# A hybrid attention and retention step on one core: where the opening stage applies the gain of its first normalisation

## The chip, the core and the metric

The kernel runs on one core of a Trainium2 chip. A core has a matrix engine (PE, TensorE), three engines that work on 128 partitions at a time (DVE, ACT and POOL: VectorE, ScalarE and GpSimd), and an engine (SP) that does little here but issue transfers. 16 DMA engines move data between the HBM and the on-chip memory SBUF. PE writes its results to PSUM, another on-chip memory, from where DVE or ACT take them; POOL works on SBUF alone. The metric is the device time of one execution in microseconds; less is better. Three runs of the kernel before had a median of 2458.14 us (2456.72 to 2460.6).

## The reference

One layer for 1024 frames of one new stream (the prompt) and 16 frames each of 8 running streams (the samples, 128 rows together). The model width is 2048; there are 8 heads of 128 for each of two branches.

```python
def rms_norm(x, g):
    y = xf * rsqrt(mean(xf * xf, axis=-1) + EPS)
    return y * g

h = rms_norm(x, norm_pre)              # (frames, 2048)
p = einsum('btd,de->bte', h, w_in)     # w_in: 2048 x 8192
q_sb, k_sb, v_sb, gate_sb, q_r, k_r, v_r, gate_r = split(p)
q_r, k_r = rope(q_r), rope(k_r) * HEAD_DIM ** -0.5
o_sb = stick_breaking_block(...)       # attention, strictly causal, over past and new keys
o_r, s = retention(...)                # 64-frame chunks and a running state
y = concat(head_norm(o_sb) * silu(gate_sb), head_norm(o_r) * silu(gate_r))
x + rms_norm(y @ w_out, norm_post)
```

The change touches only the first line of it: the mean square of a row of x, its inverse root, and the product with the 2048 gains `norm_pre`, which are the same for all rows and differ along the width.

## The kernel before

**Tiles and groups.** Nine tiles of 128 rows: eight of the prompt (0 to 7) and one of the samples (8). Group 0 holds tiles 0, 1, 2, 3 and the samples (640 columns once they are turned), group 1 tiles 4 to 7. All projections of group 0 run first, then those of group 1, then the output projection. Each projection needs h turned, with the width on the partitions: 16 blocks of 128x128 per tile.

**Products.** Both operands of a product are split into a high part (rounded by the ACT copy to the matrix engine's fp32r type) and a low part (DVE subtracts the high part from the source): `split`, L127 to L129. Three products, high by high, high by low and low by high, make one (`products`, L216 to L232; `project_rows`, L247 on). The turned and split h lies in `mov`: four parts for the width, each a pair `mh` and `ml`. The weights come as blocks `wr` of 256 KB through four buffers and are split in the same way into `wh` and `wl` (`load_w`, L207).

**The opening stage** (L335 to L402) makes `mov` for group 0:

1. `load_x` fetches a tile of x, 1 MB, into one of four buffers `xt`. The first tile is asked for first, then the gains, `norm_pre` spread over all 128 partitions as `gpre` (1 MB in two halves), then two more tiles, then the four weight blocks of the first projection, then the last two tiles. All go through SP's queue.
2. `stats` (L371): ACT squares the tile and sums the squares (`mean_square`, L350); seven small instructions on DVE and ACT make the inverse root (`inv_rms`, L131 to L142: p0v, p0r, p0u). For the first four tiles this becomes a diagonal matrix `dg` (L377); for the samples the tile itself is multiplied by it (L384).
3. Also in `stats`, the tile is multiplied by `gpre`, in eight pieces of 256 columns (L380): on POOL for tiles 1, 2 and 3 (`PRE_POOL` gives positions in the group), on DVE for tile 0 and the samples.
4. `turn` (L354): PE turns four blocks into one PSUM bank `p0t`, by a product with `dg` (L360), which scales the rows at the same time and is recorded as two instructions per block, or by a plain transpose (L358), one per block. There are four such banks.
5. `split` takes the bank apart into `mov`: ACT writes `mh`, DVE writes `ml`, both from PSUM.

After the second tile the first projection's products for the first 256 columns (L225 on 128x256) stand in the program, after all five those for the remaining 384 columns. The other columns of this first head, and `project_rows` with its blocks `wrn`, `whn`, `wln`, follow.

**Group 1** is prepared beside these products by `stage_rest` (L410 to L424), a job that moves on a step each time the products have ticked far enough: a tile is loaded and squared, one DVE instruction multiplies it by root and gains (L417), PE turns it, ACT copies the bank to `hs` (L422), and `hs` is stored in HBM for later.

**Order.** The program is traced in the order of the code, and a planner then orders each engine's instructions: it takes what its own model of the machine holds for ready, the earlier traced first. On the chip each engine keeps to that order. So an instruction that waits holds up all behind it on its engine.

Of the kernel before, what the change touches and what calls it, by code (L numbers as in the profile page):

```python
# [9 lines left out]
F32 = mybir.dt.float32  # L10
F32R = mybir.dt.float32r
AF = mybir.ActivationFunctionType
ALU = mybir.AluOpType
# [3 lines left out]
P = 128  # L17
D = 2048
KT = D // P
# [5 lines left out]
NT = PT + 1  # L25
SAMPLE = PT
WQ = 4
PRE_POOL = (1, 2, 3)
PRE_DIAG = (0, 1, 2, 3)
PRE_CUT = 8  # L30
PRE_G = 2
D_REST = 8
KC_AHEAD = 2
D_DEC = 2
# [23 lines left out]
def tile_hybrid_step(  # L58
# [26 lines left out]
    nc = tc.nc  # L85
# [12 lines left out]
    def x_rows(t):  # L98
        return x_prompt[0, t * P : (t + 1) * P, :] if t < PT else xs_flat
# [10 lines left out]
    ident = const.tile([P, P], F32, name="ident")  # L110
# [16 lines left out]
    def split(hi, lo, src):  # L127
        nc.scalar.activation(hi, src, AF.Copy)  # L128
        nc.vector.tensor_tensor(lo, src, hi.bitcast(F32), ALU.subtract)  # L129

    def inv_rms(pool, ssq, n, name):  # L131
        shape = list(ssq.shape)
        v = pool.tile(shape, F32, name=f"{name}v")
        r = pool.tile(shape, F32, name=f"{name}r")
        u = pool.tile(shape, F32, name=f"{name}u")
        nc.vector.tensor_scalar(v, ssq, 1.0 / n, EPS, ALU.mult, ALU.add)
        nc.scalar.activation(r, v, AF.Sqrt)
        nc.vector.reciprocal(r, r)
        nc.vector.tensor_tensor(u, r, r, ALU.mult)
        nc.vector.tensor_tensor(u, u, v, ALU.mult)  # L140
        nc.vector.tensor_scalar(u, u, -0.5, 1.5, ALU.mult, ALU.add)
        nc.vector.tensor_tensor(r, r, u, ALU.mult)  # L142
        return r
# [41 lines left out]
    def drain(job):  # L185
        while job is not None and not job.done:
            tick()
# [4 lines left out]
    def moving(pool, n):  # L192
        return [list(x) for x in zip(*(moving_part(pool, n, q) for q in range(KT // WQ)))]
# [42 lines left out]
    def acc_banks(g):  # L236
        return [accp.tile([P, 512], F32, name=f"acc{i}", tag=f"acc{i}") for i in range(len(g["pieces"]))]
# [9 lines left out]
    col = lambda i, h: i * H * P + h * P  # L247
# [40 lines left out]
    with ExitStack() as s1:  # L288
# [46 lines left out]
        g0 = GROUPS[0]  # L335
        with tc.tile_pool(name="p0", bufs=2) as p0, tc.tile_pool(name="p0s", bufs=1) as p0s, tc.tile_pool(
            name="p0p", bufs=4, space=PSUM
        ) as p0p:
            warm = p0s.tile([P, 1], F32, name="warm")
            nc.scalar.activation(warm, eps, AF.Sqrt)  # L340

            def load_x(t):
                xt = p0.tile([P, D], F32, name="xt", tag="xt", bufs=4)
                nc.sync.dma_start(xt, x_rows(t))
                return xt

            def mean_square(xt):
                ssq = p0.tile([P, 1], F32, name="ssq", tag="ssq")
                sq = p0s.tile([P, D], F32, name="sq0", tag="sq0")
                nc.scalar.activation(sq, xt, AF.Square, accum_out=ssq)  # L350
                return inv_rms(p0, ssq, D, "p0")

            def turn(q, xt, scale=None):
                pt = p0p.tile([P, 4, P], F32, name="p0t", tag="p0t")  # L354
                for j in range(4):
                    blk = xt[:, (4 * q + j) * P : (4 * q + j + 1) * P]
                    if scale is None:
                        nc.tensor.transpose(pt[:, j, :], blk, ident)  # L358
                    else:
                        nc.tensor.matmul(pt[:, j, :], blk, scale, start=True, stop=True)  # L360
                return pt

            tiles = g0["tiles"]
            loaded = [load_x(tiles[0])]
            gpre = p0s.tile([P, D], F32, name="gpre")
            for c in range(PRE_G):
                cs = slice(c * D // PRE_G, (c + 1) * D // PRE_G)
                nc.sync.dma_start(gpre[:, cs], norm_pre[0, cs].partition_broadcast(P))
            loaded += [load_x(t) for t in tiles[1:3]]

            def stats(i):  # L371
                xt = loaded[i]
                rstd = mean_square(xt)
                dg = None
                if i in PRE_DIAG:
                    dg = p0.tile([P, P], F32, name="dg", tag="dg")
                    nc.vector.tensor_scalar(dg, ident, rstd, None, ALU.mult)  # L377
                for c in range(PRE_CUT):
                    cs = slice(c * D // PRE_CUT, (c + 1) * D // PRE_CUT)
                    (nc.gpsimd if i in PRE_POOL else nc.vector).tensor_tensor(  # L380
                        xt[:, cs], xt[:, cs], gpre[:, cs], ALU.mult
                    )
                if dg is None:
                    nc.vector.tensor_scalar(xt, xt, rstd, None, ALU.mult)  # L384
                return dg

            scales = [stats(0)]
            for i, t in enumerate(tiles):
                if i + 1 < len(tiles):
                    scales.append(stats(i + 1))  # L390
                cs = slice(i * P, (i + 1) * P)
                for q in range(KT // 4):
                    pt = turn(q, loaded[i], scales[i])
                    split(mov[0][q][:, :, cs], mov[1][q][:, :, cs], pt)
                if i == 1:
                    w4 = list(load_w(col(4, 0)))
                    loaded += [load_x(t) for t in tiles[3:]]
                    acc = acc_banks(g0)
                    for w in w4:
                        products(mov, acc[:1], g0["pieces"][:1], *w)  # L400
            for w in w4:
                last = products(mov, acc[1:], g0["pieces"][1:], *w)  # L402

            nc.sync.dma_start(dec, c_dec)
            load_rope(0)
            with nc.allow_non_contiguous_dma(reason="small gains"):
                nc.sync.dma_start(gains[:, 0, :], sb_gain[0].rearrange("(h p) -> p h", p=P))
                nc.sync.dma_start(gains[:, 1, :], ret_gain[0].rearrange("(h p) -> p h", p=P))

            def stage_rest():  # L410
                for i, t in enumerate(GROUPS[1]["tiles"]):
                    hs = p0s.tile([P, KT, P], F32, name="hs", tag="hs")
                    xt = load_x(t)
                    yield 6

                    rstd = mean_square(xt)
                    nc.vector.scalar_tensor_tensor(xt, xt, rstd, gpre, ALU.mult, ALU.mult)  # L417
                    yield 12
                    for q in range(KT // 4):
                        with tc.issue_after(last.ins) if q == 0 else nullcontext():  # L420
                            pt = turn(q, xt)
                        nc.scalar.activation(hs[:, 4 * q : 4 * q + 4, :], pt, AF.Copy)  # L422
                        yield 3
                    nc.scalar.dma_start(s_h[:, :, i * P : (i + 1) * P], hs)  # L424

            job = Job(stage_rest(), D_REST)
            first = ret_inputs(g0, mov, 0, list(zip(acc, g0["pieces"])))
            ret_values(g0, mov, 0)
            first = *first[:2], pair["r"][:, :, 0, :], dict(rg=gate(project(g0, mov, col(7, 0)), "rg"))
            drain(job)  # L430
# [692 lines left out]
```

## Time and profile before

| | |
|---|---|
| median of 3 runs | 2458.14 us |
| the profiled execution | 2452.19 us |
| its span, first to last instruction | 2450.5 us |
| PE busy | 2372.9 us, 97% |
| DVE, ACT, POOL busy | 1263.9, 915.1, 655.6 us |
| granted PE clock over the span | 0.988 |

The span is what the engines' instructions cover; 1.7 us of the profiled execution lie outside it, and that execution is 6 us shorter than the median. PE's idle time, 78 us in all, is what a faster order can win; in the profile a row of the timeline reads: start, duration, engine, line, operation, output and input tiles with their shapes, how many, and in brackets how long the engine had been idle and what ended that. In the table of stretches each row has the busy time of an engine in the stretch and, in brackets, its number of instructions; then the granted PE clock (1 is full), the busy share of the DMA engines and what they moved.

### The profile page before, as it was taken

To read this page: it belongs to the slowest core of one execution; us is meant where nothing else is said; L and a number is where in the kernel's file an instruction comes from. 1 tells how busy PE (TensorE), PEld (TensorE's weight loads), DVE (VectorE), ACT (ScalarE), POOL (GpSimd) and SP (SyncE) were. 2 spreads that over 40 slices of the span, in tenths; PEclk is the share of its full clock that TensorE was granted. 3 is DMA by queue.
4 is the path that set the end of the run, shared out by engine and by line. 5 is a ranking of instruction groups with operands and counts; after the bars stand their busy time and mean duration, and the time that the engine had idled before them with its cause. 6 is when DMAs were issued, how large, how long until landed. Compare 5 with 4: busy or idle time off the path is not lost.

```text
span 2450.5 us, 40488 instructions
## 1 busy us (share of the span) xinstructions
PE 2372.9 (97%) x14832; PEld 2100.2 (86%) x14832; DVE 1263.9 (52%) x2434; ACT 915.1 (37%) x1931; POOL 655.6 (27%) x1029
## 2 busy tenths in 40 slices
PE   7999999999999999999889999999999998999998
PEld 7998899989999899998678888898888877878787
DVE  7245445454555555456445454545545555564544
ACT  6332333333333333334333334333433443444333
POOL 2144253444344353444102112121111211000000
PEclk9999999999999999999989999999999999999999
DMA  7659789797979798797766565566556566665553
GB/s 239 169 126 217 149 188 178 172 198 152 198 157 210 156 201 165 177 206 181 175 161 150 136 145 158 135 149 160 133 138 150 152 147 169 226 221 189 185 183 133
DMA packets 674888, 418.67 MB, mean 171 GB/s; under 512 B 224512, under 2 KB 619776, under 8 KB 672256
## 3 DMA queue, kind: packets, MB, share of 16 engines
q1 hardware_dynamic: 524272, 285.99, 48.1%
q0 software_dynamic: 32256, 71.36, 13.5%
q10 hardware_dynamic: 118160, 58.74, 8.8%
q8 instruction: 116, 1.90, 0.4%
q14 instruction: 84, 0.69, 0.1%
HBM read 336.24 MB, written 79.69 MB: 170 GB/s over the span
## 4 chain that ended last, share of the span: by engine, by line
PE 70%; issue 12%; DMA 8%; DVE 6%; POOL 2%; ACT 1%; SPq 1%; DVEq 0%; ACTq 0%; POOLq 0%
PE acc L225 33%; PE accn L274 15%; PE a L944 4%; PE a L945 4%; PE a L943 4%; PE pa L596 2%; DMA kc<-cache_sb_k 2%; DMA wr<-w_in 1%; PE z L566 1%; PE zc L639 1%; POOL kc L623 1%; DMA mr<-s_y 1%; PE pa L686 1%; DMA ro<-s_rk 1%; DVE wl L129 1%
## 5 line engine op out<-in xcount | busy, mean ns | idle before, releaser
L225 PE MATMUL acc<-mh,wh 128*128 128x256 f32 (+2 forms) x2304 | 671.8, 344 | 3.0 <-ACT wh L128 2.8
L225 PE MATMUL acc<-mh,wl 128*128 128x256 f32 (+2 forms) x2304 | 661.5, 340 | 7.4 <-DVE wl L129 7.4
L225 PE MATMUL acc<-ml,wh 128*128 128x256 f32 (+2 forms) x2304 | 666.8, 342 | 0.0
L129 DVE TENSOR_TENSOR wl<-wr,wh 128x512 fp32r<-128x512 f32 (+1 forms) x576 | 394.1, 689 | 495.4 <-ACT wh L128 479.5
L128 ACT ACTIVATE wh<-wr 128x512 fp32r<-128x512 f32 (+1 forms) x576 | 356.5, 624 | 735.5 <-PE acc L225 335.9
L225 PEld LDWEIGHTS acc<-mh,wh 128*128 128x128 f32 x2304 | 419.2, 189 | 54.4 <-issue 16.6
L225 PEld LDWEIGHTS acc<-mh,wl 128*128 128x128 f32 x2304 | 425.5, 189 | 44.9 <-DVE wl L129 10.7
L225 PEld LDWEIGHTS acc<-ml,wh 128*128 128x128 f32 x2304 | 425.5, 189 | 36.5 <-issue 9.0
L623 POOL DMA_DIRECT2D kc<-cache_sb_k x512 | 332.4, 655 | 403.0 <-DVE kcT L648 220.9
L274 PE MATMUL accn<-whn,mh 128*128 128x256 f32 x1152 | 327.8, 287 | 3.0 <-ACT mh L128 2.9
L274 PE MATMUL accn<-wln,mh 128*128 128x256 f32 x1152 | 325.3, 283 | 2.5 <-DVE wln L129 2.5
L274 PE MATMUL accn<-whn,ml 128*128 128x256 f32 x1152 | 324.7, 283 | 0.0
L274 PEld LDWEIGHTS accn<-whn,mh 128*128 128x128 f32 x1152 | 219.8, 191 | 18.7 <-issue 11.7
L944 PE MATMUL a<-wl,mh 128*128 128x512 f32 (+1 forms) x576 | 220.2, 382 | 6.7 <-DVE wl L129 6.7
L274 PEld LDWEIGHTS accn<-wln,mh 128*128 128x128 f32 x1152 | 220.6, 191 | 4.2 <-DVE wln L129 3.9
L943 PE MATMUL a<-wh,mh 128*128 128x512 f32 (+1 forms) x576 | 219.0, 382 | 2.9 <-DVE sg L301 2.4
L274 PEld LDWEIGHTS accn<-whn,ml 128*128 128x128 f32 x1152 | 220.3, 191 | 0.3 <-DVE ml L129 0.2
L945 PE MATMUL a<-wh,ml 128*128 128x512 f32 (+1 forms) x576 | 220.4, 383 | 0.0
L129 DVE TENSOR_TENSOR wln<-wrn,whn 128x512 fp32r<-128x512 f32 x128 | 87.9, 698 | 108.9 <-ACT whn L128 104.9
L491 POOL TENSOR_SCALAR_AFFINE_SELECT kp<-kp 128x128 f32<-128x128 f32 x40 | 12.4, 311 | 472.2 <-ACT kp L485 472.1
L128 ACT ACTIVATE whn<-wrn 128x512 fp32r<-128x512 f32 x128 | 78.4, 636 | 161.4 <-PE acc L225 66.5
L944 PEld LDWEIGHTS a<-wl,mh 128*128 128x128 f32 x576 | 108.7, 189 | 29.4 <-DVE wl L129 8.8
(189 smaller groups left out, 2730.5 us busy)
## 6 DMA issues: line engine op xcount, KB each, us to landing
wr<-w_in SPq DMA_DIRECT2D x384, 256.0 KB, 4.4
wr<-w_out SPq DMA_DIRECT2D x184, 256.0 KB, 3.6
wrn<-w_in SPq DMA_DIRECT2D x128, 256.0 KB, 3.3
kc<-cache_sb_k POOLq DMA_DIRECT2D x512, 64.0 KB, 5.2
vc<-cache_sb_v SPq DMA_DIRECT2D x64, 512.0 KB, 9.0
xt<-x_prompt SPq DMA_DIRECT2D x8, 1024.0 KB, 5.6
xr<-x_prompt SPq DMA_DIRECT2D x8, 1024.0 KB, 6.2
out<-out ACTq DMA_DIRECT2D x12, 512.0 KB, 2.8
```

The costliest lines, as they stand in the source:

```text
L128: nc.scalar.activation(hi, src, AF.Copy)
L129: nc.vector.tensor_tensor(lo, src, hi.bitcast(F32), ALU.subtract)
L225: last = nc.tensor.matmul(a[:, :m], lhs[:, j, :], rhs[w][:, j, o : o + m], start=(w == 0 and j == 0 and n == 0), stop=(w == KT // WQ - 1 a ...
L274: anchor[0] = nc.tensor.matmul(a, lhs[q][:, jj, ts], rhs[:, j, :], start=(w == 0 and j == 0 and n == 0 and t % 2 == 0), stop=(w == KT // 2 ...
L566: nc.tensor.matmul(z[:, :c], q2[a][:, i * P : (i + 1) * P], k2[b][:, s : s + c], start=(m == 0), stop=(m == 2),)
L596: nc.tensor.matmul(po[:, :P], at[:, j, :], vn[:, j, :], start=(j == 0), stop=(j == t))
L623: nc.gpsimd.dma_start(kc[32 * i : 32 * i + 32, :].rearrange("p (k d) -> p k d", d=32), cache_k[0, 2 * c + j, s * 512 : (s + 1) * 512, h, 3 ...
L639: nc.tensor.matmul(z[r, :], qp[:, j, r], ready[c // 2][:, c % 2, :], start=(j == 0), stop=(j == 1))
L686: nc.tensor.matmul(po[r, : 2 * P], at[:, k, r], vc[:, 2 * c : 2 * c + 2, :], start=(k == 0), stop=(k == 7))
L943: nc.tensor.matmul(a[:, :width], hi[q][:, j, ts], wh, start=(k == 0), stop=False)
L944: nc.tensor.matmul(a[:, :width], hi[q][:, j, ts], wl, start=False, stop=False)
L945: nc.tensor.matmul(a[:, :width], lo[q][:, j, ts], wh, start=False, stop=(k == KT - 1))
```

## The change

The gains no longer come as a 1 MB tile. `norm_pre` is fetched as 16 rows of 128 (`grow`, 8 KB, through ACT's queue) and turned once by PE into `gcol`, whose column k holds the gains of the width's block k, one per partition. The turned block is then multiplied by its column: `gained`, a DVE instruction from PSUM to a new SBUF tile `xg` of 128x512, of which there are two. The split works on `xg`: ACT makes the high part from it, and the low part is made by POOL for tiles 0, 2 and 3 (`PRE_POOL` is now positions 0, 2, 3) and by DVE for tile 1 and the samples. The multiplications by `gpre`, on POOL and on DVE, are gone, and all five tiles are scaled by a diagonal matrix, the samples too.

The first tile is fetched, squared and summed in two halves, which a small DVE instruction adds. Two tiles of x are asked for ahead of the weight blocks, where it was three.

In `stage_rest` DVE multiplies the tile by the root alone and takes each turned bank out itself, times its gains, where ACT copied it.

```diff
-PRE_POOL = (1, 2, 3)
-PRE_DIAG = (0, 1, 2, 3)
-PRE_CUT = 8
-PRE_G = 2
+PRE_POOL = (0, 2, 3)
...
+            def load_x(t, parts=1):
                 xt = p0.tile([P, D], F32, name="xt", tag="xt", bufs=4)
+                for c in range(parts):
+                    cs = slice(c * D // parts, (c + 1) * D // parts)
+                    nc.sync.dma_start(xt[:, cs], x_rows(t)[:, cs])
                 return xt
...
+            def mean_square(xt, parts=1):
+                ssq = p0.tile([P, parts], F32, name="ssq", tag=f"ssq{parts}")
...
+                for c in range(parts):
+                    cs = slice(c * D // parts, (c + 1) * D // parts)
+                    nc.scalar.activation(sq[:, cs], xt[:, cs], AF.Square, accum_out=ssq[:, c : c + 1])
+                if parts > 1:
+                    tot = p0.tile([P, 1], F32, name="ssqt", tag="ssqt")
+                    nc.vector.tensor_reduce(tot, ssq, mybir.AxisListType.X, ALU.add)
+                    ssq = tot
                 return inv_rms(p0, ssq, D, "p0")
+
+            def gained(dst, pt, q):
+
+                nc.vector.tensor_tensor(
+                    dst, pt, gcol[:, 4 * q : 4 * q + 4].unsqueeze(2).to_broadcast([P, 4, P]), ALU.mult
+                )
...
-            loaded = [load_x(tiles[0])]
-            gpre = p0s.tile([P, D], F32, name="gpre")
-            for c in range(PRE_G):
-                cs = slice(c * D // PRE_G, (c + 1) * D // PRE_G)
-                nc.sync.dma_start(gpre[:, cs], norm_pre[0, cs].partition_broadcast(P))
-            loaded += [load_x(t) for t in tiles[1:3]]
+            grow = p0s.tile([KT, P], F32, name="grow")
+            nc.scalar.dma_start(grow, norm_pre[0].rearrange("(k p) -> k p", p=P))
+            loaded = [load_x(tiles[0], 2), load_x(tiles[1])]
+            gcol = p0s.tile([P, KT], F32, name="gcol")
+            pt = p0p.tile([P, 4, P], F32, name="p0t", tag="p0t")
+            nc.tensor.transpose(pt[:, 0, :KT], grow, ident[:KT, :KT])
+            nc.vector.tensor_copy(gcol, pt[:, 0, :KT])

             def stats(i):
-                xt = loaded[i]
-                rstd = mean_square(xt)
-                dg = None
-                if i in PRE_DIAG:
-                    dg = p0.tile([P, P], F32, name="dg", tag="dg")
-                    nc.vector.tensor_scalar(dg, ident, rstd, None, ALU.mult)
-                for c in range(PRE_CUT):
-                    cs = slice(c * D // PRE_CUT, (c + 1) * D // PRE_CUT)
-                    (nc.gpsimd if i in PRE_POOL else nc.vector).tensor_tensor(
-                        xt[:, cs], xt[:, cs], gpre[:, cs], ALU.mult
-                    )
-                if dg is None:
-                    nc.vector.tensor_scalar(xt, xt, rstd, None, ALU.mult)
+                rstd = mean_square(loaded[i], 2 if i == 0 else 1)
+                dg = p0.tile([P, P], F32, name="dg", tag="dg")
+                nc.vector.tensor_scalar(dg, ident, rstd, None, ALU.mult)
                 return dg
...
                 for q in range(KT // 4):
-                    pt = turn(q, loaded[i], scales[i])
-                    split(mov[0][q][:, :, cs], mov[1][q][:, :, cs], pt)
+                    xg = p0.tile([P, 4, P], F32, name="xg", tag="xg")
+                    gained(xg, turn(q, loaded[i], scales[i]), q)
+                    hi, lo = mov[0][q][:, :, cs], mov[1][q][:, :, cs]
+                    nc.scalar.activation(hi, xg, AF.Copy)
+                    low = nc.gpsimd if i in PRE_POOL else nc.vector
+                    low.tensor_tensor(lo, xg, hi.bitcast(F32), ALU.subtract)
+                if i == 0:
+                    w4 = list(load_w(col(4, 0)))
+                    loaded += [load_x(t) for t in tiles[2:]]
                 if i == 1:
-                    w4 = list(load_w(col(4, 0)))
-                    loaded += [load_x(t) for t in tiles[3:]]
                     acc = acc_banks(g0)
...
                     rstd = mean_square(xt)
-                    nc.vector.scalar_tensor_tensor(xt, xt, rstd, gpre, ALU.mult, ALU.mult)
+                    nc.vector.tensor_scalar(xt, xt, rstd, None, ALU.mult)
...
-                        nc.scalar.activation(hs[:, 4 * q : 4 * q + 4, :], pt, AF.Copy)
+                        gained(hs[:, 4 * q : 4 * q + 4, :], pt, q)
```

More of the change, by code (lines that the diff above doesn't have):

```diff
@@ L340, in tile_hybrid_step @@
             nc.scalar.activation(warm, eps, AF.Sqrt)
-            def load_x(t):
+            def load_x(t, parts=1):
                 xt = p0.tile([P, D], F32, name="xt", tag="xt", bufs=4)
-                nc.sync.dma_start(xt, x_rows(t))
-                return xt
-            def mean_square(xt):
-                ssq = p0.tile([P, 1], F32, name="ssq", tag="ssq")
+                for c in range(parts):
+                    cs = slice(c * D // parts, (c + 1) * D // parts)
+                    nc.sync.dma_start(xt[:, cs], x_rows(t)[:, cs])
+                return xt
+            def mean_square(xt, parts=1):
+                ssq = p0.tile([P, parts], F32, name="ssq", tag=f"ssq{parts}")
                 sq = p0s.tile([P, D], F32, name="sq0", tag="sq0")
-                nc.scalar.activation(sq, xt, AF.Square, accum_out=ssq)
+                for c in range(parts):
[5 more added lines that the diff above has]
+                    ssq = tot
                 return inv_rms(p0, ssq, D, "p0")
+            def gained(dst, pt, q):
+                nc.vector.tensor_tensor(
+                    dst, pt, gcol[:, 4 * q : 4 * q + 4].unsqueeze(2).to_broadcast([P, 4, P]), ALU.mult
+                )
             def turn(q, xt, scale=None):
```

## The prediction

> **What bounds the kernel.** I read the page's first lines first, then the table of stretches over the opening, then the chain of waits and PE's own timeline there.
>
> ```profile
> span 2450.5 us, 40488 instructions
> PE 2372.9 (97%) x14832; PEld 2100.2 (86%) x14832; DVE 1263.9 (52%) x2434; ACT 915.1 (37%) x1931; POOL 655.6 (27%) x1029
> ```
> ```profile
> 0.00:10.00 10.00, 0.00 (x0) 0.00 (x0) 2.63 (x16) 3.69 (x5) 0.70 (x6) 1.00 0.75 288
> 10.00:20.00 10.00, 6.62 (x35) 6.46 (x36) 6.74 (x20) 6.87 (x11) 6.49 (x10) 0.93 1.08 379
> 20.00:30.00 10.00, 10.00 (x65) 10.00 (x65) 7.90 (x17) 6.99 (x11) 6.28 (x9) 0.73 0.85 252
> 30.00:40.00 10.00, 9.12 (x80) 8.88 (x78) 9.90 (x24) 6.72 (x13) 4.84 (x7) 1.00 0.64 202
> 40.00:50.00 10.00, 8.50 (x53) 7.82 (x52) 9.13 (x25) 8.81 (x15) 0.00 (x0) 1.00 0.70 234
> 50.00:60.00 10.00, 10.00 (x68) 9.98 (x67) 9.79 (x22) 5.70 (x10) 0.00 (x0) 1.00 0.35 109
> 60.00:70.00 10.00, 9.97 (x75) 9.73 (x74) 5.51 (x7) 4.31 (x8) 0.00 (x0) 1.00 0.47 138
> ```
> ```profile
> 0.81 5.02 DMA xt<-x_prompt
> ...
> 5.86 2.01 ACT sq L350 x2
> ...
> 10.33 0.29 DVE dg L377
> ...
> 44.10 15.99 PE acc L225 x99
> ```
>
> PE is busy for 97% of the span, so nearly all of the kernel goes at PE's pace, and a change to the opening can win only what PE loses there. It loses it in two ways: idle time (all of the first 10 us, 3.4 of the next, 0.9 and 1.5 in the fourth and fifth rows), and a granted clock of 0.93 and 0.73 between 10 and 30 us. From 44.10 on the chain is PE alone. So the question is by how much the moment shifts from which PE runs without a gap. PE's timeline sets the marks:
>
> ```profile
> 10.66 6.01 PE L360 MATMUL p0t<-dg,xt 128*128 128x128 f32 x32 [10.66 <-DVE dg L377]
> 19.39 6.71 PE L360 MATMUL p0t<-dg,xt 128*128 128x128 f32 x32 [2.72 <-DVE p0v L136]
> 25.86 0.36 PE L225 MATMUL acc<-mh,wh 128*128 128x256 f32 x1
> ...
> 31.68 3.74 PE L360 MATMUL p0t<-dg,xt 128*128 128x128 f32 x32
> ...
> 42.66 0.43 PE L225 MATMUL acc<-mh,wh 128*128 128x384 f32 x1
> ...
> 44.04 0.45 PE L225 MATMUL acc<-ml,wh 128*128 128x384 f32 x1
> ...
> 52.12 0.33 PE L225 MATMUL acc<-mh,wl 128*128 128x384 f32 x1
> ```
>
> Turning one tile takes PE 3.74 us at full clock (third tile) and 6.0 to 6.7 us for the first two. The first 48 products fill 25.86 to 31.68, 5.8 us. The second 48 start at 42.66, but from the second of them, at 44.04, to the last at 52.12 they run evenly; counted back by one step (0.17 us) they start in effect at 43.9. That mark is what the change moves.
>
> **The change part by part.** Prices first.
>
> ```profile
> 13.52 11.47 POOL L380 TENSOR_TENSOR xt<-xt,gpre 128x256 f32<-128x256 f32 x16 [12.13 <-ACT sq L350]
> 2183.63 2.39 POOL L1003 TENSOR_TENSOR out<-out,xr 128x1024 f32<-128x1024 f32 x1 [3.92 <-ACT out L1002]
> 2443.83 1.73 POOL L1003 TENSOR_TENSOR out<-out,xr 128x512 f32<-128x512 f32 x1 [3.98 <-ACT out L1002]
> 41.52 4.26 DVE L129 TENSOR_TENSOR ml<-p0t,mh 128x512 fp32r<-128x512 f32 x7
> L128 ACT ACTIVATE mh<-p0t 128x512 fp32r<-128x512 f32 x20 | 11.7, 597 | 7.3 <-PE p0t L360 6.2 <-PE p0t L358 0.9
> 2441.57 0.17 DVE out1v L136
> ...
> 2443.03 0.75 DVE out L1005
> ```
>
> A POOL instruction on 256 columns costs 11.47/16 = 0.72 us, on 1024 columns 2.39; on the line between them 512 columns cost 1.28. The one row with 512 shows 1.73, beside DVE instructions on the same tiles; 1.28 and 1.73 are the two ends, and I take 1.28, since it rests on two undisturbed sizes. `gained` is a DVE instruction from PSUM on 512 columns like the old `ml`: 4.26/7 = 0.61. The high part is 0.60 on ACT; from SBUF instead of PSUM I take the same. The root's chain, undisturbed at the end of the kernel, takes 2441.57 to 2443.03, 1.46 us.
>
> *The start.* Before, the square of tile 0 ends at 7.87 and `dg` starts at 10.33, 2.46 us later, because DVE's pieces of the product with `gpre` lie between the links of the chain. Without them it is 1.46: 1.0 us won. Of the square, only its second half has to follow the landing at 5.83: half of 1.91 is won less one more sum to read and the small DVE addition, together some 0.3 (both are small instructions like the chain's): 0.65, between 0.3 and 0.95. The first turn moves from 10.66 to about 9.0. DVE's copy of `gcol` stands ahead of this chain on DVE, and behind it is the whole of tile 0's root; it waits for a small transfer and one turn on PE.
>
> ```profile
> gains<-sb_head_norm SPq DMA_DIRECT2D x1, 4.0 KB, 6.5
> 11.43 1.91 ACT L350 ACTIVATE sq<-xt 128x2048 f32<-128x2048 f32 x1 [3.15 <-DMA xt<-x_prompt]
> ```
>
> A 4 KB transfer behind full tiles took 6.5 us on SP's queue. Issued on ACT's at 0.8 to 2.3 (ahead of or behind the first ACT instruction), 8 KB would land at 7.3 at the latest if issued first, and at 8.8 if issued last: 0 to 1.7 us of the gain above. With nothing ahead of it on ACT's queue I take 0.
>
> *Transfers.* The 1 MB of `gpre` is gone from between the first and second tile. In the stretch from 10 to 20 us 379 GB/s are moved, 2.8 us for 1 MB: tile 1's square can start at 8.6 instead of 11.43. One more issue on SP for the half tile (0.4 us) is off the path. The weight blocks, 1 MB too, pass the third tile, which takes `gpre`'s old place in the queue and comes no later than before.
>
> *Tiles 0 and 1.* Tile 0 again turns at the cold pace: 9.0 to 15.0. That is 1.5 us for four blocks, slower than POOL's 1.28, so the two `xg` suffice. Tile 1's root is ready by then (square 8.6 to 10.7, chain 1.46, `dg` 0.3, and up to 1.28 twice behind POOL), so PE goes straight on: 15.0 to 18.7 instead of 19.39 to 26.10. The 2.72 us that PE waited for POOL's product with `gpre` are gone, and so is the second slow stretch if the clock holds (3.0 us). Next late is the way out of PSUM. POOL ends the third group of tile 0 at about 16.1, which frees the first `xg`; then DVE owes tile 1 four times `gained` and four low parts, 8 x 0.61 = 4.9, to 21.0, plus waits of about 1. The first 48 products run behind it and end at 25.0 (22 plus the last quarter's 1.4 at the earliest, 18.7 + 5.8 = 24.5 by PE): 6.7 us earlier than 31.68.
>
> *Tiles 2, 3 and the samples.* Before, this took 31.7 to 43.9, 12.2 us. Now the samples are turned by 32 instructions, 3.74 us, and two tiles' low parts go through POOL. If PE takes tile 2 after the products, the first subtraction starts at 25.0 + 0.94 (four blocks) + 0.61 + 0.60 = 27.2; the samples' first group needs the `xg` that the seventh frees, 27.2 + 7 x 1.28 = 36.1; `gained`, high and low add 1.8, with the hops 2.0: 38.1, a gain of 5.8 on 43.9. If the planner puts part of tile 2 into PE's gaps while tile 1 is evacuated, it is bounded by PE (25.0 + 3 x 3.74 less the part already turned, 1.9, plus 1): 35.4, a gain of 8.5.
>
> *The shared waits.* Before, POOL's pieces already held DVE up:
>
> ```profile
> 19.05 0.14 DVE L136 TENSOR_SCALAR p0v<-ssq 128x1 f32<-128x1 f32 x1
> ...
> 23.81 0.69 DVE L129 TENSOR_TENSOR ml<-p0t,mh 128x512 fp32r<-128x512 f32 x1 [0.86 <-ACT mh L128]
> 24.48 1.06 DVE L129 TENSOR_TENSOR wl<-wr,wh 128x512 fp32r<-128x512 f32 x1
> ...
> 26.13 0.27 DVE L377 TENSOR_SCALAR dg<-ident,p0r 128x128 f32<-128x128 f32 x1
> ```
>
> While POOL worked, `wl`, with both inputs in SBUF, took 1.06; `ml`, with one in PSUM, kept its 0.69; and the chain of tile 2 took from 19.05 to 26.13 instead of 1.46. POOL now holds 12 x 1.28 = 15.4 us instead of 24 x 0.72 = 17.3, in longer pieces; `gained` reads PSUM and should go free, the low parts of tile 1 and the samples become SBUF instructions and join the waiting. I take 1.3 us lost from the mark (0 to 5), which cancels half of what an earlier tile 2 gives, (8.5 - 5.8)/2.
>
> The Trainium skill, page SBUF — State Buffer, section Who interferes with whom, calls this an exclusive lock held for the whole instruction, between a GpSimd instruction that reads SBUF and a DVE instruction with two SBUF inputs. The rows above agree for 0.72 us pieces; that the wait grows with the piece no run here shows. By the page every low part on DVE could lose up to a whole POOL piece, and the sum would be that of the first rival below.
>
> *`stage_rest`.*
>
> ```profile
> 48.80 2.35 DVE L417 SCALAR_TENSOR_TENSOR xt<-xt,p0r,gpre 128x2048 f32<-128x2048 f32 x1
> 39.65 1.27 DVE L384 TENSOR_SCALAR xt<-xt,p0r 128x2048 f32<-128x2048 f32 x1
> L422 ACT ACTIVATE hs<-p0t 128x512 f32<-128x512 f32 x16 | 9.6, 597 | 12.6 <-PE p0t L358 11.8 <-DVE rk L312 0.7
> ```
>
> Per tile DVE gets 1.27 + 4 x 0.61 - 2.35 = 1.4 us more, ACT 2.4 us less. The 1.1 us taken off come where DVE is full (9.79 of 10 us in 50 to 60), the 2.4 added come behind the turns, from 60 us on, where DVE has 4.5 us free in the next ten. Priced at nothing; without that cover it costs 4 x 1.4 = 5.6 us.
>
> *Sum.* 5.8 + 1.3 - 1.3 = 5.8 us off the profiled execution's 2452.19: 2446.4. That execution lies 6 us under the median of the runs; against the median, 2458.14 - 5.8 = 2452.3.
>
> **The rivals.**
>
> *POOL and DVE get in each other's way.* With the contended price of 1.73 the seventh subtraction ends at 27.2 + 12.1 = 39.3 and the mark is at 41.3; a gain of 2.6, less some waits, 2 us: 2456. For it speaks the row with 1.73 and that the split of the weights falls into the same time; against it that DVE's `gained` reads PSUM.
>
> *Slower: the evacuation of `stage_rest` on DVE.* ACT waited 11.8 us for PE's turns before its 16 copies, 0.74 each. DVE would now wait so, in order, with the low parts of the next weight blocks queued behind it, and PE waiting for those. It decides from the point at which a wait is longer than the lead of the weights' split over the products. If each wait reaches PE, 11.8 us are lost against 5.8 gained: 6 slower, 2464. Against it: DVE is only 5.51 us busy in 60 to 70 and can run ahead.
>
> *The gain doesn't arrive.* What PE wins is given back at the next wait, 2458. Against it stands that PE is full from 50 us on, with nothing to absorb a lead.
>
> **How the numbers follow.** A change of less than 0.2%, 4.9 us, can't be told from none here. The forecast has 0.48; its own range is 4.3 to 8.5 us gained, 2449.6 to 2453.9. POOL against DVE has 0.27, slower 0.17, no arrival 0.08. Faster by over 0.2%: 0.45 of the forecast and 0.05 of POOL against DVE, 0.50. Slower 0.17, within 0.2% the remaining 0.33. The range goes from 2447, a little under the PE bound for the run-to-run spread, to 2462.5, half way into the slow case.
>
> **What would show it.** Right: first turn on `dg` near 9.0; no PE gap between tiles 0 and 1; the first products near 19 to 20; L225 on 128x384 even from about 38; POOL rows of 512 columns at 1.3 us; no PE idle between 50 and 100. Wrong: POOL rows near 1.7, a granted clock well under 1 past 20 us, DVE's `gained` into `hs` followed by late `wln` and PE idle, or an order by the planner that puts tile 2 last.

## The result and the profile after

The changed kernel is slower: 2464.63 us median of seven runs (2463.32 to 2471.07) against 2458.14 (2455.52 to 2460.6), a ratio of 1.0035 with a 95% interval of 1.0024 to 1.0046, or 8.6 us (5.9 to 11.3); the medians alone lie 6.5 us apart. The forecast was 5.8 us less than before. From the page of the changed kernel:

```profile
span 2465.8 us, 40525 instructions
PE 2378.4 (96%) x14849; PEld 2103.3 (85%) x14849; DVE 1271.8 (52%) x2444; ACT 906.5 (37%) x1917; POOL 654.0 (27%) x1017
```

The two profiled executions lie further apart than the medians, 15.3 us by span: that of before was 6 us under its median, that of after 3 us over its own. So the spans are no measure. The marks in the opening are sharper: tile 1's first turn starts at 19.57 to 19.65 us in the changed kernel and in the four versions below (e1, e3, e4, e5) that leave the order ahead of it alone. The table of stretches, cut at PE's marks (first turn; end of tile 0's turns; tile 1's first turn; end of the first 48 products; start of the even run of the second 48; their end), first of the changed kernel, then of the kernel before:

```profile
0.00:9.59 9.59, 0.25 (x1) 0.17 (x2) 1.96 (x13) 4.44 (x8) 0.70 (x6) 1.00 0.81 269
9.59:14.98 5.39, 5.39 (x32) 5.20 (x32) 3.20 (x8) 4.56 (x9) 1.41 (x2) 1.00 1.11 374
14.98:19.57 4.59, 0.00 (x1) 0.03 (x1) 4.59 (x9) 2.89 (x4) 3.23 (x3) 1.00 0.97 359
19.57:31.82 12.25, 12.25 (x91) 12.18 (x92) 9.91 (x30) 7.78 (x14) 1.05 (x1) 0.86 0.82 231
31.82:48.69 16.87, 11.24 (x89) 10.08 (x88) 13.85 (x22) 11.36 (x18) 11.03 (x8) 0.95 0.45 147
48.69:59.29 10.60, 10.60 (x48) 10.60 (x48) 8.60 (x25) 5.99 (x12) 0.00 (x0) 0.76 0.33 118
```
```profile
0.00:10.66 10.66, 0.00 (x1) 0.00 (x1) 3.29 (x18) 3.69 (x5) 0.70 (x6) 1.00 0.77 298
10.66:16.67 6.01, 6.00 (x32) 5.81 (x32) 2.98 (x8) 4.04 (x7) 3.15 (x5) 1.00 1.11 352
16.67:19.39 2.72, 0.01 (x1) 0.04 (x1) 2.62 (x7) 2.28 (x5) 2.72 (x5) 0.86 1.03 413
19.39:31.68 12.29, 12.29 (x80) 12.29 (x81) 9.97 (x24) 8.50 (x14) 8.57 (x13) 0.75 0.88 272
31.68:44.04 12.36, 9.97 (x84) 9.06 (x82) 12.36 (x27) 8.87 (x16) 3.17 (x4) 1.00 0.60 196
44.04:52.30 8.26, 8.26 (x49) 8.26 (x48) 7.39 (x21) 7.77 (x12) 0.00 (x0) 1.00 0.52 171
```

Row by row: 1.1 us won at the start, 0.6 in tile 0 (the same 32 turns take 5.34 to 6.76 us in those four versions, so this row isn't the change's), 1.9 lost in waiting for tile 1, nothing in the fourth row, 4.5 lost in tiles 2, 3 and the samples, 2.3 lost in the second products, which ran at a granted clock of 0.76. Together 7.0 us later, of 8.6 (5.9 to 11.3). PE's own timeline of the changed kernel, where the number in brackets is PE's idle time:

```profile
9.59 5.39 PE L371 MATMUL p0t<-dg,xt 128*128 128x128 f32 x32 [4.88 <-DVE dg L386]
19.57 5.44 PE L371 MATMUL p0t<-dg,xt 128*128 128x128 f32 x32 [4.59 <-issue]
...
31.82 5.30 PE L371 MATMUL p0t<-dg,xt 128*128 128x128 f32 x46
38.36 2.02 PE L371 MATMUL p0t<-dg,xt 128*128 128x128 f32 x16 [1.24 <-DVE xg L360]
41.01 2.38 PE L371 MATMUL p0t<-dg,xt 128*128 128x128 f32 x16 [0.63 <-DVE xg L360]
45.07 1.16 PE L371 MATMUL p0t<-dg,xt 128*128 128x128 f32 x8 [1.68 <-DVE xg L360]
...
48.69 0.66 PE L222 MATMUL acc<-ml,wh 128*128 128x384 f32 x1 [1.85 <-DVE ml L400]
```

Behind the opening the shift stands for a while as it is: the first `pa` product on `rv` starts at 140.6 us before and at 147.5 in the changed kernel, 6.9 later.

For the experiments one mark serves for the whole opening: the start of the first `project_rows` product, `accn`, 15.0 to 15.9 us behind the end of the second products. It is the first number behind "to" of these rows' durations (before, changed kernel, and the last of the versions below but one):

```profile
L274 PE MATMUL accn<-whn,mh x51: 278/283/368, 68.2 to 89.8; 128*128 128x256 f32 x51
```
```profile
L271 PE MATMUL accn<-whn,mh x37: 278/283/364, 75.1 to 89.9; 128*128 128x256 f32 x37
```
```profile
L271 PE MATMUL accn<-whn,mh x63: 278/283/368, 63.8 to 89.6; 128*128 128x256 f32 x63
```

| version | start of `accn`, us | against before, us | ratio of times to before (95% interval) |
|---|---|---|---|
| before | 68.2 | | |
| changed kernel | 75.1 | +6.9 | 1.0035 (1.0024 to 1.0046) |
| e1, four `xg` | 69.2 | +1.0 | 1.0003 (0.9987 to 1.0019) |
| e2, POOL without low parts | 74.2 | +6.0 | 1.0036 (1.0020 to 1.0052) |
| e3, `stage_rest` later | 72.4 | +4.2 | 1.0032 (1.0016 to 1.0047) |
| e4, `stage_rest` as before | 74.8 | +6.6 | 1.0040 (1.0023 to 1.0057) |
| e5 = e1 + e3 | 67.0 | -1.2 | 1.0001 (0.9988 to 1.0015) |
| e6 = e1, weights later | 66.0 | -2.2 | 0.9995 (0.9982 to 1.0008) |
| e7 = e1, POOL in half pieces | 67.3 | -0.9 | 1.0004 (0.9986 to 1.0023) |
| e8, before with a halved first tile | 68.1 | -0.1 | 1.0004 (0.9991 to 1.0016) |
| e9, tile 1's root first | 72.8 | +4.6 | 1.0013 (1.0004 to 1.0023) |
| e10, all four mends | 63.8 | -4.4 | 0.9986 (0.9975 to 0.9997) |
| e11 = e10, POOL in half pieces | 68.6 | +0.4 | 1.0002 (0.9987 to 1.0017) |

The mark and the ratio go together: 0.1% is 2.5 us, and each ratio's interval takes in its mark's shift. Yet a mark is that of one execution, and PE's clock alone can shift it: the stretch from tile 1's first turn to the first product took 5.92 us in e1, at a granted clock of 0.58, and 3.56 in e7, at 1.00, for the same turns. So each step below is read in its own stretch, and what the clock did is said beside it.

### The profile page after: what moved, and what is told of

It is laid out like the page before. It is cut to its first block, busy times and chain, and to the rows that moved or that the text cites. A ratio compares the mean times of both kernels' runs of the same rounds, so it can differ in the third digit from the quotient of the medians.

```text
span 2465.8 us, 40525 instructions
## 1 busy us (share of the span) xinstructions
PE 2378.4 (96%) x14849; PEld 2103.3 (85%) x14849; DVE 1271.8 (52%) x2444; ACT 906.5 (37%) x1917; POOL 654.0 (27%) x1017
## 4 chain that ended last, share of the span: by engine, by line
PE 57%; issue 12%; DMA 8%; DVE 5%; POOL 2%; ACT 1%; SPq 1%; DVEq 0%; POOLq 0%; ACTq 0%
PE acc L222 25%; PE accn L271 12%; PE a L951 4%; PE a L952 4%; PE a L950 4%; PE pa L603 2%; DMA kc<-cache_sb_k 1%; PE z L573 1%; POOL kc L630 1%; DMA mr<-s_h 1%; DMA wr<-w_in 1%; DMA ro<-s_rk 1%; DMA mr<-s_y 1%; PE zc L646 1%; PE pa L693 1%
## 5 line engine op out<-in xcount | busy, mean ns | idle before, releaser
L498 POOL TENSOR_SCALAR_AFFINE_SELECT kp<-kp 128x128 f32<-128x128 f32 x40 | 12.4, 310 | 484.0 <-ACT kp L492 483.8
```

## The experiments

Three theories stood at the start, and a fourth came after the first results: POOL's long subtractions hold up DVE's instructions with two inputs in SBUF (A); two `xg` are too few (B); `stage_rest`'s DVE work gets in ahead of the samples (C); what DVE is given ahead of tile 1's root keeps PE idle (D, the later one).

**e1: four buffers.**

```diff
-xg = p0.tile([P, 4, P], F32, name="xg", tag="xg")
+xg = p0.tile([P, 4, P], F32, name="xg", tag="xg", bufs=4)
```

> The changed kernel with four xg buffers instead of two. In the changed kernel the second 48 products end at 59.3 us (52.3 before); between 31.8 and 48.7 us PE stood idle for 5.6 us, 3.6 of it put down to DVE's gained, which waits for POOL to free an xg. Theory B (the two buffers are what is too few): DVE no longer waits for POOL between tiles 2, 3 and the samples, the idle time between 31.8 and the samples falls by 3 us or more, the clock stays up, and the products end near 54; total 4 to 6 us under the changed kernel. Theory A (the port that POOL and DVE share holds DVE up): the buffers change little, the same two-input DVE instructions wait, products end within 1.5 us of 59.3. Theory C (stage_rest's own DVE work stands ahead of the samples): the gain is at most 2 us.

The second products ended at 53.35, the ratio went from 1.0035 to 1.0003. That is B's number: 4.8 of the 5.9 us come in the stretch of tiles 2, 3 and the samples (12.1 us instead of 16.9), and 1.5 in the second products, at a clock of 1.00 instead of 0.76, less 0.3 lost ahead of them. POOL's timeline of the changed kernel shows what two buffers did:

```profile
34.81 2.51 POOL L400 TENSOR_TENSOR ml<-xg,mh 128x512 fp32r<-128x512 f32 x2 [1.62 <-ACT mh L398]
38.95 2.49 POOL L400 TENSOR_TENSOR ml<-xg,mh 128x512 fp32r<-128x512 f32 x2 [1.63 <-ACT mh L398]
41.69 2.50 POOL L400 TENSOR_TENSOR ml<-xg,mh 128x512 fp32r<-128x512 f32 x2 [0.25 <-ACT mh L398]
45.76 2.24 POOL L400 TENSOR_TENSOR ml<-xg,mh 128x512 fp32r<-128x512 f32 x1 [1.56 <-ACT mh L398]
```

Groups go in pairs: POOL subtracts two, then DVE fills a buffer, ACT copies it, and in three of the four gaps POOL stands idle for 1.6 us. A buffer that is free isn't filled at once: the first of the pair of 34.81 was free at about 36.1, but DVE was at another instruction until 37.6, longer than its usual 0.41 us while POOL worked:

```profile
36.10 1.51 DVE L309 TENSOR_TENSOR rq<-rq,sw 128x256 f32<-128x256 f32 x1
```

With four, POOL and PE of e1 run through:

```profile
37.37 7.92 POOL L400 TENSOR_TENSOR ml<-xg,mh 128x512 fp32r<-128x512 f32 x6 [0.65 <-ACT mh L398]
```
```profile
32.16 10.21 PE L371 MATMUL p0t<-dg,xt 128*128 128x128 f32 x90
```

**e2: no low part on POOL.**

```diff
-PRE_POOL = (0, 2, 3)
+PRE_POOL = ()
```

> The changed kernel with all low parts on DVE, none on POOL: DVE gets 12 x 0.61 = 7.3 us more work, POOL none, and xg is freed without POOL. Theory A (port): tile 1's root no longer waits behind subtractions of 1.28 us, dg of tile 1 starts at about 15 instead of 18.18, so PE's 4.6 us of idle time ahead of tile 1 falls to about 1; the waits of 1.2 to 2.2 us of DVE instructions on one column are gone; the second products end at 55 or less. Theory B (buffers): an xg is held 0.6 us for the low part instead of 1.28, so it gains too, but only after 31.8; tile 1 still starts near 19.5. If DVE's sheer work is the bound instead, the products end later than 59.3, by up to 7.

The first turn of tile 1 came at 17.16, 2.4 us earlier, and the first products ended at 28.64, 3.2 us earlier; the stretch behind them took 19.1 us instead of 16.9, and the second products ended at 58.66. So A holds for 2.4 us ahead of tile 1, not for the whole 4.6, and DVE's sheer work took it back: in that stretch DVE of e2 is busy for 17.26 of 19.08 us.

```profile
28.64:47.72 19.08, 13.40 (x98) 12.41 (x96) 17.26 (x39) 12.63 (x21) 0.00 (x0) 0.91 0.47 145
```

**e3: `stage_rest` planned later.** Each of its squares gets an order-only tie to the last of the second products (`last`).

```diff
-rstd = mean_square(xt)
+rstd = mean_square(xt, after=last)
...
+if after is not None:
+    tc.add_manual_dep(ins.ins, after.ins.name, <order only>, reason="behind the products")
```

> The changed kernel with stage_rest's squares (and so roots and scalings) planned behind the last of the second products. In the changed kernel a root and a scaling of group 1's first tile stand on DVE at 42.1 to 46.9 ahead of the samples' low parts. Theory C: those 4 to 5 us go, the second products start near 44.5 instead of 48.7 and end at 54 to 55; total 4 us less. Theories A and B: only what these few instructions cost themselves goes, about 2 us, and tile 1 still starts at 19.5.

The even run of the second products started at 47.04, 1.7 us earlier, and they ended at 56.58, 2.7 earlier: 1.5 us come in the stretch of tiles 2, 3 and the samples (15.3 us instead of 16.9), and 1.1 in the second products, which took 9.54 us at a clock of 0.85 instead of 10.60 at 0.76. So C accounts for some 1.5 us, less than its 4 to 5. In the total it can't be told from the changed kernel. The rows that went, from the changed kernel's DVE:

```profile
42.28 0.71 DVE L136 TENSOR_TENSOR p0u<-p0r 128x1 f32<-128x1 f32 x1
43.02 1.19 DVE L137 TENSOR_TENSOR p0u<-p0u,p0v 128x1 f32<-128x1 f32 x1
...
45.60 1.28 DVE L424 TENSOR_SCALAR xt<-xt,p0r 128x2048 f32<-128x2048 f32 x1
```

These belong to group 1, whose turns come at 67 us. The planner put them ahead of the samples, and two of them, 0.71 and 1.19 us long where such an instruction takes 0.16, run while POOL works.

**e4: `stage_rest` as before**, with `gpre` fetched behind the tiles of x.

```diff
-nc.vector.tensor_scalar(xt, xt, rstd, None, ALU.mult)
+nc.vector.scalar_tensor_tensor(xt, xt, rstd, gpre, ALU.mult, ALU.mult)
...
-gained(hs[:, 4 * q : 4 * q + 4, :], pt, q)
+nc.scalar.activation(hs[:, 4 * q : 4 * q + 4, :], pt, AF.Copy)
```

> The changed kernel with only stage_rest as it was (product with a gpre tile, loaded behind the tiles of x, and ACT's copy): undoes that part alone. If DVE's way out of PSUM in stage_rest costs time behind the opening (the slower rival of the prediction), the total falls by 3 us or more with the opening unchanged at 59.3. If the loss sits in the opening, the products end within 2 us of 59.3 (DVE's 2.35 us instruction may stand where 1.28 stood) and the total stays within 3 us of the changed kernel.

Nothing came back: second products' end at 59.81, ratio 1.0040. The slower rival of the prediction, DVE's way out of PSUM in `stage_rest`, is out.

**e5: e1 and e3 together.**

> Four xg buffers and stage_rest planned behind the second products, together. Alone they brought the end of the second products from 59.3 to 53.4 and to 56.6. If the two losses are separate, the end falls to 51 to 52, at or just under the kernel before (52.3), and the total is even with it or 1 to 2 us less. If they are the same loss seen twice (the samples' groups late on DVE), it stays at 53 to 54.

51.11, 2.2 us less than e1: separate losses. 0.7 of the 2.2 lie ahead of the end of the first products, in tile 1's turns at a clock of 0.67 instead of 0.58; the other 1.5 come behind it, as in e3.

**e6: e1, and the weight blocks asked for and split where the kernel before had them**, with three tiles ahead.

```diff
 if i == 0:
-    w4 = list(load_w(col(4, 0)))
-    loaded += [load_x(t) for t in tiles[2:]]
+    loaded += [load_x(tiles[2])]
 if i == 1:
+    w4 = list(load_w(col(4, 0)))
+    loaded += [load_x(t) for t in tiles[3:]]
```

> Four xg buffers, and the weight blocks of the first projection asked for and split where the kernel before had them, behind the second tile and after the third tile's transfer. In the changed kernel the four low parts wl (0.61 us each, up to 1.8 with the wait for POOL) stand between the links of tile 1's root on DVE. Theory D (what DVE is given ahead of the links of tile 1's root keeps PE idle from 15.0 to 19.6): the first turn of tile 1 comes 2 to 3 us earlier than 19.6. Theory A (the wait for POOL alone): it stays within 1 us of 19.6, since POOL's subtractions are where they were. The first products start later or at the same time as 25.5, because the weights' split is later; so the end of the second products is within 2 us of 53.4.

Tile 1's first turn came at 18.37, 1.2 us earlier: between the two theories' numbers. The first products did not start later but at 23.57 (25.51 in e1), and the second ended at 50.12, 3.2 us earlier than in e1, more than expected; 0.7 of it is again the clock in tile 1's turns (0.67 instead of 0.58). So asking for the weights earlier cost time, which suggests that their transfers were not what was late; what in the earlier order cost the other 2.5 us, the transfers or the splits that follow them, this run doesn't tell apart.

**e7: e1 with POOL in half pieces.**

```diff
-low.tensor_tensor(lo, xg, hi.bitcast(F32), ALU.subtract)
+for k in (0, 2) if i in PRE_POOL else (0,):
+    ks = slice(k, k + 2) if i in PRE_POOL else slice(0, 4)
+    low.tensor_tensor(lo[:, ks, :], xg[:, ks, :], hi[:, ks, :].bitcast(F32), ALU.subtract)
```

> Four xg buffers, and POOL's low parts in two pieces of 256 columns (0.72 us each in the kernel before) instead of one of 1.28: the same work with a shorter hold of the port, at 0.16 us more per group. Theory A: the waits of DVE's two-input instructions halve, tile 1's first turn comes 1 us or more earlier than 19.6 and the second products end at 52 or less. If the length of the hold doesn't matter, all stays within 0.5 us, plus up to 1.3 us for POOL's extra time in tiles 2 and 3.

Tile 1 came at 19.01, 0.6 us earlier, with PE's first turn 1.0 us later (10.61); the second products ended at 51.48. That is in direction A, and the links of tile 1's root were held for less: 0.68 and 0.74 us where e1 has 1.22 and 1.29. But the 1.9 us at the second products are no proof of it: tile 1's turns, at a clock of 1.00 where e1 had 0.58, took 2.4 us less, more than the whole gain, and the planner's order changed with the count of instructions too.

**e8: the kernel before with its first tile in two halves**, as in the change.

> The kernel before with one part of the change alone: the first tile fetched, squared and summed in two halves. The prediction gave this part 0.65 us (0.3 to 0.95) at the start. In the changed kernel the two squares of 1.06 us, with 0.19 each, ended at 7.56 with the tile landed at 6.4, against 7.87 before: expected 0.3 us or less, first turn between 10.2 and 10.7, total the same within what can be told.

The halves alone win nothing beside `gpre`: the first turn came at 11.08 instead of 10.66, outside the expected 10.2 to 10.7. The first half had landed only at 5.14 (the whole tile before at 5.83), and ACT was busy with its square until the second could start at 6.38; the first link of the root came 0.14 us earlier than before, at 7.75 instead of 7.89. Then the product with `gpre` stood waiting for its row to land, until 8.40. From e8's ACT and its DVE:

```profile
5.14 1.06 ACT L354 ACTIVATE sq<-xt 128x1024 f32<-128x1024 f32 x1 [2.83 <-DMA xt<-x_prompt]
```
```profile
8.40 0.42 DVE L388 TENSOR_TENSOR xt<-xt,gpre 128x256 f32<-128x256 f32 x1 [0.50 <-DMA gpre<-norm_pre]
```

**e9: the changed kernel with tile 1's root ahead of tile 0's way out**, on DVE; `made[1]` is the instruction that makes tile 1's diagonal matrix.

```diff
-gained(xg, turn(q, loaded[i], scales[i]), q)
+pt = turn(q, loaded[i], scales[i])
+with tc.issue_after(made[1].ins) if i == 0 else nullcontext():
+    gained(xg, pt, q)
```

> The changed kernel with one thing moved: on DVE the way out of PSUM of tile 0 (four gained) stands behind tile 1's diagonal matrix, so that no link of tile 1's root waits for a turn of tile 0 or for POOL. The weights' low parts still stand among the links. Theory D (DVE's order around tile 1's root keeps PE idle for 4.6 us): tile 1's first turn comes at 15 to 16 instead of 19.6, the first products end near 29 instead of 31.8. Behind that the two xg buffers are as few as before, so the second products end 1 to 3 us earlier, 56 to 58, not the full 4. If the root's lateness is not what holds tile 1, it stays at 19.6.

PE of e9 goes straight from tile 0 into tile 1, 48 instructions without a gap, and then stands still, twice for an `xg`:

```profile
9.53 8.47 PE L371 MATMUL p0t<-dg,xt 128*128 128x128 f32 x48 [4.87 <-DVE dg L386]
19.66 2.39 PE L371 MATMUL p0t<-dg,xt 128*128 128x128 f32 x16 [1.66 <-DVE xg L360]
24.50 2.65 PE L371 MATMUL p0t<-dg,xt 128*128 128x128 f32 x16 [2.45 <-DVE xg L360]
```

So D names what held tile 1's first turn. But the expectation missed: the first products ended at 33.74, not near 29, because two buffers are too few for tiles 0 and 1 as well. The mark is 2.3 us earlier all the same.

**e10: all four mends** (e1, e3, e6, e9).

> All four mends together: four xg buffers, stage_rest planned behind the second products, the weight blocks where the kernel before had them, and tile 1's root ahead of tile 0's way out. Apart they gave (end of the second products) 59.3 to 53.4, to 51.1 with stage_rest, to 50.1 with the weights. If the mends add: tile 1's first turn at 15, the first products' end near 28, the second products' end at 47 to 48, 4 to 5 us under the kernel before, and a total 0.1 to 0.2% under it. If POOL's eight subtractions of tiles 2 and 3 (10.2 us) have become the bound behind the first products, the end is not under 49.

The second products ended at 47.93, the first at 28.28; ratio 0.9986 (0.9975 to 0.9997, just clear of 1), 3.4 us less than the kernel before. From e10's PE, its DVE, and its last stretch:

```profile
9.59 9.37 PE L378 MATMUL p0t<-dg,xt 128*128 128x128 f32 x64 [4.91 <-DVE dg L393]
```
```profile
10.99 0.15 DVE L133 TENSOR_SCALAR p0v<-ssq 128x1 f32<-128x1 f32 x1 [1.37 <-ACT sq L351]
...
12.38 0.29 DVE L393 TENSOR_SCALAR dg<-ident,p0r 128x128 f32<-128x128 f32 x1
```
```profile
39.70:47.93 8.23, 8.23 (x48) 8.23 (x49) 5.42 (x8) 4.48 (x6) 1.00 (x1) 1.00 0.53 183
```

Tiles 0 and 1 are turned in one run of 64, tile 1's root takes 1.4 us, and the clock is 1.00 throughout the opening: those 64 turns take 9.37 us, where the kernel before took 6.01 and 6.71.

**e11: e10 with POOL in half pieces.**

> The same with POOL's low parts in two pieces of 256 columns. In the changed kernel with four buffers this moved the first products' end from 32.2 to 29.4, because DVE's two-input instructions waited less. With tile 1's root already out of POOL's way that gain is spent: expected within 1 us of the version with whole pieces, and POOL's 16 pieces cost it up to 1.3 us behind the first products.

Slower by 4.8 us at the mark, where 1 was expected. POOL took 12.19 us instead of 10.56 for tiles 2 and 3, and their stretch was 1.0 us longer, as expected. Most of the rest is the clock, 0.85 in the stretch of the first products and 0.83 in that of the second, where e10 had 1.00: PE was busy there for 8.47 and 9.83 us instead of 7.00 and 8.23, 3.1 us more. So this run says little against half pieces.

## Why the prediction was wrong

**Where it failed first: "PE goes straight on", tile 1 at 15.0.** It came at 19.57. The prediction let the links of tile 1's root run as an undisturbed chain with two waits. On DVE of the changed kernel they stand in line:

```profile
11.71 0.69 DVE L360 TENSOR_TENSOR xg<-p0t,gcol 128x512 f32<-128x512 f32 x1 [2.09 <-PE p0t L371]
...
13.84 0.75 DVE L136 TENSOR_TENSOR p0u<-p0r 128x1 f32<-128x1 f32 x1
...
15.12 1.21 DVE L137 TENSOR_TENSOR p0u<-p0u,p0v 128x1 f32<-128x1 f32 x1
...
17.58 0.68 DVE L126 TENSOR_TENSOR wl<-wr,wh 128x512 fp32r<-128x512 f32 x1
18.18 1.29 DVE L386 TENSOR_SCALAR dg<-ident,p0r 128x128 f32<-128x128 f32 x1
```

`dg` starts at 18.18 where e10 has it at 12.38. Behind the first `gained`, which waited for a turn, the chain shares DVE with three more `gained` and three of the four `wl`, and three links (0.75, 1.21 and 1.29 us) last longer beside POOL. e2 takes 2.4 us off, e6 1.2, e9 and e10 the whole. The same fault of reading was in the profile before: there too the root of tile 1 was done only at 18.41, its matrix at 19.13, and the prediction charged PE's wait until 19.39 to POOL's product alone:

```profile
18.41 0.72 DVE L377 TENSOR_SCALAR dg<-ident,p0r 128x128 f32<-128x128 f32 x1
```

It also showed tile 2's chain taking from 19.05 to 26.13 and charged that to POOL, but six `ml` and `wl` stand there between the links, and the links themselves take 0.14 to 0.68 us.

The end of the first products came at 31.82, where 25.0 was predicted. 4.6 of these 6.8 us are the late start of tile 1. Then 12.25 us passed, not 10.0: the clock was 0.50 from 19.71 to 23.12, so that tile 1's turns took 5.44 us, not 3.74. The 3.0 us that the prediction gave to them "if the clock holds" became 1.3. PE's row there:

```profile
19.71:23.12 3.41, 3.41 (x17) 0.50 0.85 204
```

**Where it failed most: "so the two `xg` suffice", and 7 x 1.28 without a gap.** The price held: the first seven subtractions of tiles 2 and 3 took 1.25 to 1.27 us each. But the sum laid seven of them end to end, and with two buffers they took 12.3 us from the first start to the last end, 3.5 of it in gaps. Tiles 2, 3 and the samples took 16.9 us, where 13.1 were predicted and 12.4 measured before. The first subtraction even started 2.1 us sooner behind the first products than in the sum, since part of tile 2 had been turned; behind the seventh 4.5 us passed instead of 2.0, with the scaling of `stage_rest` (1.28 us) and an `ml` of 1.70 in between. Four buffers bring the stretch to 12.1 (e1).

**A term that was missing: the clock.** The loss of the last row, 2.3 us, is the clock alone: PE was busy throughout in both kernels. It fell behind a stretch in which PE worked in short bursts (last section). The prediction's sum has the clock only in tiles 0 and 1, though a clock well under 1 past 20 us is among its signs of being wrong.

**A place that was missed: `stage_rest`.** "Priced at nothing" was right for the way out of PSUM (e4) and missed that the shorter scaling and its roots would be moved up into the opening, some 1.5 us (e3, e5).

**The small steps.** The start: 9.0 predicted, 9.59 measured; the 1.0 us from the product with `gpre` was right (1.47 us from the root's first link to `dg`, 2.44 before), the 0.65 from the halves was 0.1 (the first link at 7.78 instead of 7.89; e8 agrees). The wait for `gcol`: nothing, as taken; the row was there at 4.46, and its copy ran behind `dg`, not ahead of the chain. Tile 0: 6.0 predicted, 5.39. Part of tile 2 was indeed turned among the first products, ten of its 32 instructions. Putting the weights ahead of the third tile was priced at nothing and cost some 2.5 us beside four `xg` (e6 against e1).

**The rivals.** Slower came true by none of the mechanisms given for it. POOL against DVE was real, but the contended row of 1.73 was not its form: POOL's rows stayed at 1.25 to 1.47, but for the last, 2.24, which began just behind DVE's scaling at 45.60; DVE waited, with up to 1.2 us for an instruction that takes 0.16. That is what the Trainium skill's page SBUF — State Buffer says in its section Who interferes with whom, a hold for the whole instruction; 1.21 and 1.29 against 0.16 and 0.29 agree, now for pieces of 1.28 to 1.47. In e2, with POOL idle, no link of tile 1's root took more than 0.16, and `dg` took 0.28.

What stays open: 8.6 us (5.9 to 11.3) were measured, 6.5 by the medians, and 7.0 are found in the opening; the rest is within the interval. How much of the 7.0 the clock takes in the mean of many executions is not shown either, with one trace of each version.

## What to carry to other kernels

A sum of stage prices holds only where buffers allow the stages to overlap: count how long a buffer is held through all engines that pass it on (here 0.6, 0.6 and 1.28 us, 2.5 in all) against the pace of the slowest. Two buffers allow one group per 1.25 us, just POOL's 1.28, with nothing left for the moments in which DVE is at something else; a pair that is barely enough on paper was too few. A chain of tiny instructions on an engine that keeps its order costs what stands between its links; moving such a chain ahead, and tying work that isn't due behind the work that is, together with two more buffers and the weights' old place, turned a loss of 0.35% into a gain of 0.14% with no operation removed. And before pricing the parts of a change together, ask which of them the profile wants at all: the halved tile won 0.1 us, and the earlier weights did harm.

## What the runs showed of the hardware

PE's clock was halved without a long pause. From the changed kernel, stretches of 3.4 us:

```profile
43.60:47.00 3.40, 1.60 (x9) 1.00 0.01 5
47.00:50.40 3.40, 1.71 (x5) 0.50 0.88 304
50.40:53.80 3.40, 3.40 (x12) 0.50 0.04 12
```

In the first, PE was busy for 1.60 us, its longest pause there being under 1.9; then the clock was 0.5 for two stretches, though PE worked through the second of them, and the products that started at 48.69 ran at half speed until 53.8. The Trainium skill, page TensorE: Matmul & The Clock Gate, section Why this matters for your kernels, asks for no idle gap over about 3 us; here the clock fell with none over 1.9. In e7 it stayed at 1.00 behind a pause of 3.06 us ahead of tile 1.

The cut at 3.4 us is not arbitrary: in the openings of these traces the clock stays at a value for 3.41 us or a multiple of it. Where these stretches fall differs from trace to trace, and it matters. Ahead of the even run of the second products PE paused for 1.54 us in e11 and for 1.57 in e7. In e11 it lay within one stretch; in e7 a border, at 41.08, divides it. First e11, then e7:

```profile
40.69:44.11 3.42, 1.69 (x8) 1.00 0.81 271
44.11:47.52 3.41, 3.41 (x13) 0.50 0.25 103
```
```profile
17.19:20.60 3.41, 1.59 (x14) 1.00 0.92 328
41.08:44.50 3.42, 2.23 (x12) 1.00 0.70 278
44.50:47.91 3.41, 2.67 (x16) 1.00 0.04 7
```

The clock fell behind a stretch with 1.60 us busy (changed kernel), 1.69 (e11) and 1.43 (kernel before, 15.24 to 18.65), and not behind e7's with 2.23 and 2.67; but e7's first row, with 1.59, was followed by 1.00 too. So short bursts of PE may lose the clock or may not, and what decides it these runs don't show.
